# Experts' weights loaded 2 MB at a time, into a ring with two more 1 MB places

## The chip, the cores and the metric

The program runs on one core of a Trainium2 chip. The metric is the device time of one execution in microseconds, the median of several runs.

## The reference

Two transformer blocks follow each other on 256 tokens of 1024 features, in float32. The first has two layers of attention and MLP. The second mixes latent attention with a bidirectional mLSTM and ends in a layer of 16 experts, whose weights are the largest part of what is read:

```python
def ec_moe(x, w_router, w_e_gate, w_e_up, w_e_down):
    B, T, D = x.shape
    cap = CAP_FACTOR * T // N_EXPERTS
    aff = jax.nn.softmax((x @ w_router).astype(jnp.float32), axis=-1)
    g, idx = lax.top_k(aff.transpose(0, 2, 1), cap)
    xs = jax.vmap(lambda xb, ib: xb[ib])(x, idx)
    a = jnp.einsum('becd,edf->becf', xs, w_e_gate)
    u = jnp.einsum('becd,edf->becf', xs, w_e_up)
    y = jnp.einsum('becf,efd->becd', jax.nn.silu(a) * u, w_e_down) * g[..., None].astype(x.dtype)
    ...
```

Each of the 16 experts takes its 32 best tokens (cap = 32), and has three matrices of 1024 x 1024: 201 MB together, all of which is read once.

## The kernel before

**The parts.** The first block and the mixer of the second come first. Their weights arrive 1 MB at a time in the four buffers `wr` (`load_w`), ACT rounds them to a high part (`whi`), DVE or Pool takes the rest (`wlo`), and TensorE makes three products of each with the high and low parts of x. Then come the router and the experts.

**The experts.** They are worked in four groups of four (G4 = 0 to 3). Each group has 16 tiles of gate weights, 16 of up and 16 of down; a tile holds 128 rows and 512 columns of each of the four experts, 128 x 2048 floats or 1.049 MB. In all there are 192 tiles, numbered here 0 to 191 in the order in which they are used (`order_e`): 0 to 15 are the first group's gate, 16 to 31 its up, 32 to 47 its down, and so on. `product` makes four products of a tile, one per expert, with no rounding in between. TensorE's order is written by hand; the other engines' is set by a scheduler that keeps to the program's dependences.

**Between gate and up of the first group.** First only the rows of the first four experts are gathered (`xs0`), a feature tile ahead of each two gate tiles. After gate tile 15 the rows of the other twelve are gathered (`xsr`, eight feature tiles of 384 columns), then the slots' tokens are transposed (`ptr`) and their gates taken (`gsl`), and only then comes tile 16, the first of up.

**The ring of places.** `load_e` issues the loads of the tiles on SP's queue, in the order of use; each waits in that queue until the place that it goes to is free. `slots` names 23 places for the first 23 tiles, in the order in which they become free: the buffers of parts that are done. Some are whole (a row of a partition is 8 KB), some are put together of two halves of 4 KB rows (`("ew2.h0", "ew2.h4")`). From tile 23 on the places are used again in turn, `again`: all of them but the two that lie in `xsr` and the two named `once`, which other things need later. So 19 places go round, 14 whole and 5 halved:

```python
again = [s for s in slots if not any(p.startswith(("xsr", "once")) for p in s)]
...
s = slots[i] if i < len(slots) else again[(i - len(slots)) % len(again)]
```

**The end.** The last group's down tiles are laid out by columns, 128 at a time, so that little is left after the last load, which comes in four parts; then the last norm and four stores.

Of the kernel before, what the change touches and what calls it, by code (L numbers as in the profile page):

```python
# [16 lines left out]
PIECE = 512  # L17
# [25 lines left out]
LAST = (4, 2, 1, 1)  # L43
HP = 40
# [89 lines left out]
def lay_out(i):  # L134
# [10 lines left out]
    # the four rows of its block on each row  # L145
# [16 lines left out]
    # every q, then every k, then every v  # L162
# [27 lines left out]
    w = g["w_e_down_2"][0, 12:].reshape(4, 2, 4, 128, 8, 128).transpose(4, 1, 3, 2, 0, 5)  # L190
    o["w_e_down"][48:] = w.reshape(16, 128, 2048)
# [4 lines left out]
class Filler:  # L196
    """Matrix-product work that may run whenever the tensor engine would wait for another engine."""
# [42 lines left out]
def fused_kernel(ctx: ExitStack, tc: tile.TileContext, I, out):  # L240
# [26 lines left out]
    # brings the table of exp and tanh in while the first loads run  # L267
# [86 lines left out]
    def three(o, wh, wl, xh, xl, st, sp):  # L354
        mm(o, wh, xh, st, False)
        mm(o, wh, xl, False, False)
        mm(o, wl, xh, False, sp)

    def w_stationary(v, xs, o, small=0, ks=0, first=True, last=True):
        """o[:, m*256:(m+1)*256] (one bank) (+)= W[:, m-tile].T @ x over the contraction tiles of v"""  # L360
        xh, xl = xs
        K, n = v.shape[1], v.shape[2]
        for k0, k1, _, hv, lv in pieces(v, small):
            for k in range(k0, k1):
                for m in range(n // 128):
# [29 lines left out]
    def accumulate(w, dn, xh, xl, kx, first, last):  # L395
        """dn (8 output tiles in four banks) += W[two contraction tiles].T @ x[kx:kx+2]"""
        def one(k, m, hv, lv, m0, kk):
            ms = slice((m - m0) * 128, (m - m0 + 1) * 128)
            three(dn[m // 2][:, (m % 2) * 256:(m % 2) * 256 + 256], hv[:, kk, ms], lv[:, kk, ms], xh[:, kx + k],
                  xl[:, kx + k], first and k == 0 and m % 2 == 0, last and k == 1)  # L400

        if last:
            # finish one output tile after the other
# [20 lines left out]
    def heads_apart(u, d):  # L424
        """of two heads on 64 rows each: hi and lo above one another, hi where the head is"""
# [14 lines left out]
    def rstd_cols(ssum, n, nm, bank=None):  # L440
        """per token (partition) 1/sqrt(mean + eps), for the two token tiles"""
# [11 lines left out]
    def bcast_rows(col2, dst, bank=None):  # L453
        """dst[p, t*128 + s] = col2[s, t] on every partition"""
# [6 lines left out]
    def updated(dn):  # L461
        """x += dn, two tiles of features at a time"""
# [27 lines left out]
    with tc.tile_pool(name="memp", bufs=1) as mp:  # L490
# [15 lines left out]
        def mem_side(l, o, w):  # L506
            mh = mp.tile([128, 8, 256], FR, tag="mh", name="mh", bufs=2)
            ml = mp.tile([128, 8, 256], FR, tag="ml", name="ml", bufs=2)
            g = w_stationary(w, (mh, ml), o, 0 if l else 2)
# [4 lines left out]
            return mh, ml  # L514
# [36 lines left out]
    # ------------------------------------------------------------ first block  # L551
# [3 lines left out]
    def layer(l, lp, ap, start):  # L555
        hh, hl, ssum = start
        xs = (hh, hl)
        stat = {}

        # blocks of two heads, feature-major: the first kind's q, the second's, their k  # L560
# [4 lines left out]
        def tables():  # L565
            """the turns of q and k, with the norm's factor"""
# [10 lines left out]
        def turned(c, o):  # L577
            """rotates two blocks, each dimension with the one eight rows away"""
# [154 lines left out]
        def pv_dil():  # L733
# [3 lines left out]
            # the two heads in turn, each on its half of the columns of the array  # L737
# [86 lines left out]
        def project(mp_):  # L824
# [22 lines left out]
        for mp_ in range(4):  # L847
            project(mp_)
            if mp_:
                accumulate(load_w(I["w_out"][l, mp_ - 1]), dn, yh, yl, 2 * mp_ - 2, mp_ == 1, False)  # L850
        accumulate(load_w(I["w_out"][l, 3]), dn, yh, yl, 6, False, True)
        return dn

    def mlp(l, mp, side, dn):
        # what is used last lies where the last products' operands still are
        urs = [mp.tile([128, 2, 256], FT, name=f"ur{i}") for i in range(2)]
        uhs, uls = ([mp.tile([128, 2, 256], FR, name=f"u{n}{i}") for i in range(LAG + 1)] for n in "hl")
        hh, hl, ssum = split_and_sum(dn, ("g_mlp", l * 8), mp, () if l else HMQ)
# [4 lines left out]
        def up(c):  # L863
            o = acc_tile("up")
            return o, w_stationary(load_w(I["w_up"][l, c]), (hh, hl), o)

        def relu2(o):
            r = urs[nu[0] % 2]
            uh, ul = uhs[nu[0] % (LAG + 1)], uls[nu[0] % (LAG + 1)]
# [4 lines left out]
            return uh, ul  # L874
# [6 lines left out]
        for c in range(1, 16):  # L881
# [18 lines left out]
    def silu_row(v):  # L900
        """twice the silu"""
# [4 lines left out]
    def mod_rows(a, b, vs, mp):  # L906
        """columns of the modulation as sums along the rows of their weights"""
# [10 lines left out]
    def modulation(mp):  # L918
        """shift and scale of both sides"""
# [19 lines left out]
    # ------------------------------------------------------------ second block  # L939
# [14 lines left out]
    def modulated(src, rb, sc, sh, tp, emit, eng=None):  # L954
        """emit(k, t, shift column): h[k] = t + shift, t = src*rstd*scale"""
# [54 lines left out]
    def queries(xs, kpe, qn, qp, tp):  # L1010
# [4 lines left out]
        qh = tp.tile([128, 3, 256], FR, tag="qh", name="qh")  # L1015
        ql = tp.tile([128, 3, 256], FR, tag="ql", name="ql")
# [19 lines left out]
        for c in (2, 0, 1):  # L1036
# [24 lines left out]
    def gate_weights(wg, tp):  # L1061
        """the gates' weights for xc and xm themselves, through the blocks of q, k and v"""
# [15 lines left out]
        # q meets k through the product of their blocks  # L1078
# [13 lines left out]
    def diagonals(n, i):  # L1092
        """the 4x4 blocks of each tile of features on the diagonal of a square"""
# [78 lines left out]
    def log_gates(gt, gc, tp):  # L1172
        """gc: a, b, total, largest a"""
# [21 lines left out]
    def rows(gc, t):  # L1195
        """the rows a of a tile on every partition"""
# [783 lines left out]
```

## Time and profile before

| what | us |
|---|---|
| median of 3 runs | 1614.09 (1611.87 to 1615.5) |
| span of the profiled execution, first to last instruction | 1614.4 |
| TensorE busy (matrix products) | 1444.0 |
| DVE, ACT, Pool busy | 895.1, 674.2, 234.1 |

The page gives the profiled execution by its span; it has no other time of its own. A busy share is an average over parts with different limits, so the experts' part has to be read by itself: by the slices of the page, by windows and by timelines. In those the `gate`, `up` and `y` products read `ew`, the tile of weights; `ew` loads on SPq (SP's queue) are the experts' loads. A line L288 or L1660 is that of a helper, so groups are told apart by their tiles.

### The profile page before, as it was taken

How to read it: one execution, taken by the hardware profiler on the slowest of the kernel's cores; microseconds unless marked ns; L12 is line 12 of the kernel's file. 1: busy time of each engine (PE TensorE's matmuls, PEld its weight loads, DVE VectorE, ACT ScalarE, POOL GpSimd, SP SyncE). 2: the span in 40 equal slices, each digit the busy share in tenths (PEclk: the TensorE clock that was granted, in tenths of full speed). 3: DMA queues.
4: the chain of work that ended last, by engine and by line, in shares of the span. 5: the costliest groups of instructions: out<-in, count | busy, mean ns of one | idle time of the engine just before them, and what ended most of it. 6: DMA issues, size and time to landing. Idle time of an engine off the chain costs nothing.

```text
span 1614.4 us, 27279 instructions
## 1 busy us (share of the span) xinstructions
PE 1444.0 (89%) x10903; PEld 1153.8 (71%) x10903; DVE 895.1 (55%) x1609; ACT 674.2 (42%) x1339; POOL 234.1 (14%) x204
## 2 busy tenths in 40 slices
PE   8999999999999999999988999999798666766766
PEld 7999999999998998999987899878642100110114
DVE  7876688776886588897698875954410000000001
ACT  7555555555556556555565665544310000000001
POOL 3100022212210015322153101300100000000000
PEclk9999999999999999999999999999899788877787
DMA  8543446666443456767743322544889999999997
GB/s 310 186 142 131 158 170 254 243 227 217 183 157 115 160 196 229 273 253 273 274 162 111 132 79 98 196 183 156 339 345 416 419 419 418 418 417 417 419 418 320
DMA packets 67119, 404.89 MB, mean 251 GB/s; under 512 B 7344, under 2 KB 9264, under 8 KB 26544
## 3 DMA queue, kind: packets, MB, share of 16 engines
q1 hardware_dynamic: 66848, 403.04, 65.2%
q8 instruction: 85, 1.39, 0.3%
q14 instruction: 42, 0.34, 0.1%
q10 hardware_dynamic: 144, 0.11, 0.0%
HBM read 402.08 MB, written 1.05 MB: 250 GB/s over the span
## 4 chain that ended last, share of the span: by engine, by line
PE 61%; issue 29%; DVE 6%; ACT 2%; POOL 1%; DMA 0%; SPq 0%; POOLq 0%; ACTq 0%; DVEq 0%
PE dn L288 13%; PE up L288 10%; PE gate L288 9%; PE tanh L288 4%; PE z L288 4%; PE v L288 2%; PE prj L288 2%; DVE wlo L351 2%; PE scl L288 2%; PE wo L288 1%; PE sc L288 1%; DVE pre L1112 1%; PE xm L288 1%; PE S L288 1%; PE pvl L288 1%
## 5 line engine op out<-in xcount | busy, mean ns | idle before, releaser
L345 ACT CAST whi<-wr 128x512 fp32r<-128x512 f32 (+1 forms) x647 | 394.2, 616 | 366.7 <-PE up L288 81.1
L351 DVE TENSOR_TENSOR wlo<-wr,whi 128x512 fp32r<-128x512 f32 (+1 forms) x563 | 404.3, 728 | 158.5 <-ACT whi L345 156.3
L349 POOL TENSOR_TENSOR wlo<-wr,whi 128x512 fp32r<-128x512 f32 (+1 forms) x84 | 119.4, 1422 | 487.7 <-ACT whi L345 446.8
L288 PE MATMUL up<-hh,wlo 128*128 128x256 f32 x512 | 146.0, 285 | 6.0 <-DVE wlo L351 4.8
L288 PE MATMUL up<-hl,whi 128*128 128x256 f32 x512 | 145.6, 284 | 1.3 <-DVE hl L421 1.2
L1898 DVE TENSOR_TENSOR ehh<-up,ehh 128x512 f32<-128x512 f32 x8 | 5.5, 692 | 253.1 <-PE up L288 253.1
L288 PE MATMUL dn<-uh,wlo 128*128 128x256 f32 x512 | 145.3, 284 | 0.4 <-DVE wlo L351 0.4
L288 PE MATMUL up<-hh,whi 128*128 128x256 f32 x512 | 145.4, 284 | 0.2 <-ACT whi L345 0.2
L288 PE MATMUL dn<-uh,whi 128*128 128x256 f32 x512 | 145.0, 283 | 0.0
L288 PE MATMUL dn<-ul,whi 128*128 128x256 f32 x512 | 144.9, 283 | 0.0
L288 PE MATMUL y<-ew,ehl 128*32 128x128 f32 (+1 forms) x896 | 91.0, 512 | 39.5 <-DMA ew<-in_w_e_down_dram 38.6
L288 PE MATMUL up<-ew,xsr 128*32 128x512 f32 x384 | 82.1, 811 | 39.3 <-DMA ew<-in_w_e_up_dram 39.3
L288 PE MATMUL gate<-hh,whi 128*128 128x256 f32 x384 | 110.0, 286 | 0.0
L288 PE MATMUL gate<-hl,whi 128*128 128x256 f32 x384 | 108.6, 283 | 0.0
L288 PE MATMUL gate<-hh,wlo 128*128 128x256 f32 x384 | 108.6, 283 | 0.0
L288 PE MATMUL gate<-ew,xsr 128*32 128x512 f32 x384 | 71.0, 706 | 37.1 <-DMA ew<-in_w_e_gate_dram 36.7
L288 PEld LDWEIGHTS up<-hh,wlo 128*128 128x128 f32 x512 | 98.1, 192 | 8.1 <-DVE wlo L351 6.6
L288 PEld LDWEIGHTS up<-hl,whi 128*128 128x128 f32 x512 | 98.1, 192 | 2.4 <-DVE hl L421 2.1
L288 PEld LDWEIGHTS y<-ew,ehl 128*32 128x32 f32 x896 | 28.4, 128 | 99.0 <-DMA ew<-in_w_e_down_dram 77.4
L288 PEld LDWEIGHTS dn<-uh,wlo 128*128 128x128 f32 x512 | 98.3, 192 | 0.9 <-DVE wlo L351 0.8
L288 PEld LDWEIGHTS up<-hh,whi 128*128 128x128 f32 x512 | 98.1, 192 | 0.4 <-ACT whi L345 0.4
L288 PEld LDWEIGHTS dn<-uh,whi 128*128 128x128 f32 x512 | 98.3, 192 | 0.1
(531 smaller groups left out, 3477.9 us busy)
## 6 DMA issues: line engine op xcount, KB each, us to landing
ew<-in_w_e_down_dram SPq DMA_DIRECT2D x47, 1024.0 KB, 16.1
ew<-in_w_e_gate_dram SPq DMA_DIRECT2D x46, 1024.0 KB, 15.6
ew<-in_w_e_up_dram SPq DMA_DIRECT2D x46, 1024.0 KB, 15.7
wr<-in_w_up_dram SPq DMA_DIRECT2D x32, 1024.0 KB, 4.8
wr<-in_w_down_dram SPq DMA_DIRECT2D x32, 1024.0 KB, 5.9
wr<-in_w_gates_dram SPq DMA_DIRECT2D x24, 1024.0 KB, 4.8
wr<-in_w_modT_dram SPq DMA_DIRECT2D x24, 1024.0 KB, 4.9
wr<-in_w_in_dram SPq DMA_DIRECT2D x24, 1024.0 KB, 4.8
```

Source lines behind the costliest of these rows:

```text
L288: PE.matmul(o, l, r, start=st, stop=sp, skip_group_check=True)
L345: A.copy(hv, src)
L349: behind[1] = G.tensor_tensor(lv, src, hv.bitcast(FT), op=OP.subtract).ins
L351: behind[0] = V.tensor_tensor(lv, src, hv.bitcast(FT), op=OP.subtract).ins
L1112: V.scalar_tensor_tensor(pre, xm[:, k, w:w + 256], vc("cw", w * 8 + k), pre, op0=OP.mult, op1=OP.add)
L1898: V.tensor_tensor(h[:, c], up[j], h[:, c], op=OP.mult)
```

## The change

It does five things.

1. The program is built with `dynamic_dma_scratch_size=64`: the room that Pool's descriptors have in SBUF, which this kernel does not use, becomes free, 16 KB of each partition. A new pool `ew0` there holds two places of 1 MB, `("ew0.a/0",)` and `("ew0.a/1",)`, first in `slots`. `load_e(2)` fills them long before the other loads of experts, where the second block begins. So `slots` has 25 places.
2. Tiles of equal size that lay apart are made in pairs (`hi_lo`, `whl.w`, `x2p.xh`, `x2p.hx`, `yp.y`, `ew1.e`), so that two places of 1 MB lie side by side in each.
3. On the host, the experts' weights are laid out with two tiles side by side, 32 blocks of 128 x 4096, so that a partition's row of two tiles is 16 KB.
4. From tile 25 on only the five pairs of places in `again` are used, and two tiles are loaded by one transfer of 2 MB. Tile 25 itself, and the last four (`TAIL`), are loaded alone, the very last in four parts as before.
5. Comments and docstrings go. The helpers take the pair of hi and lo as one tile.

```diff
+TAIL = 4
...
     for n in ("gate", "up", "down"):
-        w = g["w_e_%s_2" % n][0].reshape(4, 4, 8, 128, 2, 512).transpose(0, 2, 4, 3, 1, 5)
-        o["w_e_" + n] = np.ascontiguousarray(w).reshape(64, 128, 2048)
+        w = g["w_e_%s_2" % n][0].reshape(4, 4, 8, 128, 2, 512).transpose(0, 2, 3, 4, 1, 5)
+        o["w_e_" + n] = np.ascontiguousarray(w).reshape(32, 128, 4096)
...
-    whi = whl.tile([128, WH * PIECE], FR, tag="whi", name="whi")
-    wlo = whl.tile([128, WH * PIECE], FR, tag="wlo", name="wlo")
+    whx = whl.tile([128, 2, WH * PIECE], FR, tag="w", name="wh")
+    whi, wlo = whx[:, 0], whx[:, 1]
...
+    def hi_lo(pl, K, tag, **kw):
+
+        t = pl.tile([128, 2, K, 256], FR, tag=tag, name=tag, **kw)
+        return t[:, 0], t[:, 1], t
...
-        load_e(2 + E1)
+        load_e(4 + E1)
...
+    slots = ([("ew0.a/0",), ("ew0.a/1",), ("yp.y/0",), ("yp.y/1",), ("ew1.e/0",), ("ew1.e/1",), ("ew1.f",)] +
+             [("ew2.h0", "ew2.h4"), ("ew2.h1", "ew2.h5"), ("ew2.h6",), ("ew2.h2", "ew2.h8"), ("cst.cbuf2", "ew2.h9"),
+              ("ew2.h3", "ew2.h10"), ("xsr.0",), ("ew2.h11", "xsr.1"), ("x2p.xh/0",), ("x2p.xh/1",)] +
+             [("wrp.wr",)] * WR + [("whl.w/0",), ("whl.w/1",), ("x2p.hx/1",), ("once.xT",)])
+
+    again = ["ew0.a", "yp.y", "ew1.e", "x2p.xh", "whl.w"]
...
+    def load_e(upto):
+        while len(ring) < min(upto, len(order_e)):
+            i = len(ring)
+            G4, n, q = order_e[i]
+            src = I["w_e_" + n][G4 * 8 + q // 2][:, q % 2 * 2048:q % 2 * 2048 + 2048]
+            if i < len(slots):
+                parts = slot_parts(i)
+                w = 2048 // len(parts)
+                for j, t in enumerate(parts):
+                    load_part(t, src[:, j * w:(j + 1) * w])
+                ring.append(parts)
+                continue
+            t = halves(again[(i - len(slots) + 1) // 2 % len(again)])
+            if q % 2 == 0 and i < len(order_e) - TAIL:
+                load_part(t.rearrange("p a n -> p (a n)"), I["w_e_" + n][G4 * 8 + q // 2])
+                ring.extend([[t[:, 0]], [t[:, 1]]])
+            else:
+                parts = [t[:, q % 2]]
...
+    pools["ew0"] = pool(yst, "ew0", "right")
+    yp = pools["yp"] = pool(yst, "yp", "right")
+    load_e(2)
...
-    nc = _bacc.Bacc("TRN2", target_bir_lowering=False, num_devices=1)
+    nc = _bacc.Bacc("TRN2", target_bir_lowering=False, num_devices=1, dynamic_dma_scratch_size=64)
```

**Where the loads stand: the first places used again.** SP's queue, before, from the last tile of the first filling (`xT`, tile 22) on. A number behind `ew` is the place's; `128x1024` is a half.

```order
L1660 DMA xT_84<-in_w_e_up_dram 128x2048 [waits DMAHW5_49,DVE_49,PE_49]
L1660 DMA ew_12892<-in_w_e_up_dram 128x2048 [waits DMAHW6_49,PE_49]
L1660 DMA ew_12898<-in_w_e_up_dram 128x2048 [waits DMAHW7_49,PE_49]
L1660 DMA ew_12904<-in_w_e_up_dram 128x2048 [waits DMAHW0_49,PE_49]
L1660 DMA ew_12910<-in_w_e_up_dram 128x2048 [waits DMAHW1_49,PE_49]
L1660 DMA ew_12940<-in_w_e_up_dram 128x2048 [waits DMAHW2_49,PE_49]
L1660 DMA ew_12946<-in_w_e_up_dram 128x1024 [waits DMAHW3_49,PE_49]
```

The same place of SP's queue now, from the last tile of the first filling (`xT`, tile 24) on. ew_9091 is `ew0.a`, ew_11737 `yp.y`, ew_11740 `ew1.e`, ew_12414 `x2p.xh`, ew_12624 `whl.w`.

```order
L1492 DMA xT_84<-in_w_e_up_dram 128x2048 [waits DMAHW7_49,DVE_49,PE_49]
L1492 DMA ew_9091<-in_w_e_up_dram 128x2048 [waits DMAHW0_49,PE_49]
L1492 DMA ew_11737<-in_w_e_up_dram 128x4096 [waits DMAHW1_49,PE_49]
L1492 DMA ew_11740<-in_w_e_up_dram 128x4096 [waits DMAHW2_49,PE_49]
L1492 DMA ew_12414<-in_w_e_up_dram 128x4096 [waits DMAHW3_49,PE_49]
L1492 DMA ew_12624<-in_w_e_down_dram 128x4096 [waits DMAHW5_49,DMAHW4_49,PE_49]
L1492 DMA ew_9091<-in_w_e_down_dram 128x4096 [waits DMAHW0_49,PE_49]
```

Before, a new place per tile, each that of the next tile used. Now tile 25 goes alone, tiles 26 and 27 to `yp.y`, 28 and 29 to `ew1.e`, 30 and 31 to `x2p.xh`, 32 and 33 to `whl.w`, 34 and 35 to `ew0.a` again.

**Who reads those places.** TensorE, now, from the last gate tile (15) to the second up tile (17).

```order
L289 MATMUL gate1_12678<-ew_12414,xs0_12676 32x512 x4
L289 MATMUL xs_12776<-P_12671,ew_12627 128x384 x2
...
L289 MATMUL xs_12804<-P_12671,ew_12627 128x384 x2
L1870 MATMUL ptr_12809<-cbuf_81,P_12671 128x128 x4
L1870 MATMUL ptr_12815<-cbuf_81,P_12671 128x128 x4
L289 MATMUL gsl_12821<-aff_12641,P_12671 128x4 x8
L289 MATMUL up0_12833<-ew_12414,xs0_12676 32x512 x4
L289 MATMUL up1_12834<-ew_12616,xs0_12676 32x512 x4
```

And before, at the same point.

```order
L288 MATMUL gate1_12703<-ew_12639,xs0_12701 32x512 x4
L288 MATMUL xs_12801<-P_12696,ht_12671 128x384 x2
...
L288 MATMUL gsl_12848<-aff_12665,P_12696 128x4 x8
L288 MATMUL up0_12860<-ew_12641,xs0_12701 32x512 x4
L288 MATMUL up1_12861<-ew_12643,xs0_12701 32x512 x4
```

TensorE's order is the same. The two halves of `x2p.xh` (ew_12414) now hold tile 15 and tile 16, on either side of the gathers; before, tile 15 lay in a buffer of `wr` of its own.

**The two early loads.** SP's queue now, where the second block begins; before, the same rows stand there without the two of `ew_9091`.

```order
L316 DMA wr_9193<-in_w_in2_dram 128x2048 [waits DMAHW2_49,DVE_49,Pool_49]
L316 DMA wr_9280<-in_w_in2_dram 128x2048 [waits DMAHW3_49,DVE_49]
L316 DMA wr_9355<-in_w_in2_dram 128x8x128 [waits DMAHW4_49,DVE_49]
L1492 DMA ew_9091<-in_w_e_gate_dram 128x2048 [waits DVE_49]
L1492 DMA ew_9091<-in_w_e_gate_dram 128x2048
L316 DMA wr_9401<-in_w_ukv_dram 128x2048 [waits DMAHW5_49,DVE_49,Pool_49]
```

On ACT two activations of silu (L1892 before, on `gate`) now stand among the eight copies of the gathers into `xsr`, instead of behind them.

## Rows read from the trace of the kernel before

**Rows 1.** The page's 40 slices of 40.4 us: DMA busy tenths, GB/s.
```profile
DMA  8543446666443456767743322544889999999997
GB/s 310 186 142 131 158 170 254 243 227 217 183 157 115 160 196 229 273 253 273 274 162 111 132 79 98 196 183 156 339 345 416 419 419 418 418 417 417 419 418 320
```

**Rows 2.** Waits of TensorE from 1000 us: us in total, times, longest.
```profile
PE up L288 <- DMA ew<-in_w_e_up_dram: 39.3, 53, 2.4
PE y L288 <- DMA ew<-in_w_e_down_dram: 38.6, 42, 1.9
PE gate L288 <- DMA ew<-in_w_e_gate_dram: 36.7, 48, 1.6
```

**Rows 3.** Windows: rows of 8 KB alone, of 4 KB alone, the whole stream.
```profile
core 0: us, PE busy (x) PEld busy (x) DVE busy (x) ACT busy (x) POOL busy (x), PEclk, DMA share, GB/s
...
1255.00:1282.00 27.00, 17.43 (x94) 2.62 (x92) 0.00 (x0) 0.53 (x1) 0.00 (x0) 0.81 1.01 421
...
1389.00:1395.00 6.00, 4.10 (x20) 0.59 (x20) 0.00 (x0) 0.00 (x0) 0.00 (x0) 1.00 1.02 408
1176.40:1604.30 427.90, 309.91 (x2034) 79.65 (x2033) 20.90 (x34) 17.80 (x34) 0.00 (x0) 0.84 1.01 415
```

**Rows 4.** Timeline of SP's queue: start, us, what; the last first filling, the first reuse.
```profile
1159.12 0.33 SPq L1660 DMA_DIRECT2D xT<-in_w_e_up_dram  x1
1175.36 14.14 SPq L1660 DMA_DIRECT2D ew<-in_w_e_up_dram  x12
```

**Rows 5.** Windows of 5 us around the start of the stream.
```profile
1165.00:1170.00 5.00, 0.00 (x0) 0.00 (x0) 4.72 (x12) 0.00 (x0) 1.01 (x1) 0.50 0.39 165
1170.00:1175.00 5.00, 4.16 (x18) 2.53 (x22) 2.05 (x6) 0.46 (x1) 0.00 (x0) 0.50 0.00 0
1175.00:1180.00 5.00, 5.00 (x44) 1.87 (x40) 0.41 (x1) 0.46 (x1) 0.00 (x0) 0.99 0.74 254
1185.00:1190.00 5.00, 5.00 (x44) 1.88 (x40) 0.41 (x1) 0.46 (x1) 0.00 (x0) 1.00 1.00 407
1190.00:1195.00 5.00, 5.00 (x35) 2.09 (x28) 0.63 (x1) 0.00 (x0) 0.00 (x0) 1.00 1.00 366
```

**Rows 6.** Timeline of the end: the last product of experts, the stores.
```profile
1604.62 1.08 PE L288 MATMUL y<-ew,ehl 128*32 128x128 f32 x32
...
1609.18 1.81 SPq L1957 DMA_DIRECT2D out_dram<-yo  x4
```

**Rows 7.** Timeline of TensorE, first group: start, us; a tile is 8 records.
```profile
1173.45 2.70 PE L288 MATMUL gate<-ew,xs 128*32 128x512 f32 x16
...
1176.72 1.92 PE L288 MATMUL gate<-ew,xs 128*32 128x512 f32 x16
...
1179.22 1.92 PE L288 MATMUL gate<-ew,xs 128*32 128x512 f32 x16
...
1192.77 10.59 PE L288 MATMUL xs<-P,ht 128*128 128x384 f32 x32
...
1204.61 1.93 PE L288 MATMUL gsl<-aff,P 128*128 128x4 f32 x16
1206.81 5.36 PE L288 MATMUL up<-ew,xs 128*32 128x512 f32 x48 [0.27 <-DVE gs L1852]
...
1224.84 11.37 PE L288 MATMUL y<-ew,ehl 128*32 128x512 f32 x104
1237.22 1.06 PE L288 MATMUL y<-ew,ehl 128*32 128x512 f32 x8 [1.01 <-DMA ew<-in_w_e_down_dram]
```

**Rows 8.** SP's queue and a window where the second block begins.
```profile
798.46 11.45 SPq L315 DMA_DIRECT2D wr<-in_w_in_dram  x4
813.21 0.34 SPq L315 DMA_DIRECT2D wr<-in_w_ukv_dram  x1
...
800.00:820.00 20.00, 19.39 (x162) 19.19 (x161) 16.50 (x27) 11.21 (x24) 9.21 (x9) 1.00 0.66 233
```

**Rows 9.** Groups of ACT by line and form, 1290 to 1615 us: count, busy, mean ns.
```profile
L1892 ACT ACTIVATE ehh<-gate 128x512 f32<-128x512 f32 x4 | 2.4, 597 | 158.2 <-PE gate L288 158.2
```

More of the change, by code (lines that the diff above doesn't have):

```diff
@@ L366, in w_stationary @@
                     ms = slice(m * 128, (m + 1) * 128)
-                    three(o[:, m * 256:(m + 1) * 256], hv[:, k - k0, ms], lv[:, k - k0, ms], xh[:, ks + k],
-                          xl[:, ks + k], first and k == 0 and m == 0, last and k == K - 1)
+                    three(o[:, m * 256:(m + 1) * 256], hv[:, k - k0, ms], lv[:, k - k0, ms], x2[:, :, ks + k],
+                          first and k == 0 and m == 0, last and k == K - 1)
                 yield 0.33 * (n // 128)
     def x_stationary(v, xs, os_, ks=None, first=True, last=True):
-        xh, xl = xs
+        xh, xl = xs[:2]
         K, n = v.shape[1], v.shape[2]
@@ L393, in out_banks, with accumulate @@
         return [dw[j // 2][:, (j % 2) * 512:(j % 2) * 512 + 512] for j in range(4)]
-    def accumulate(w, dn, xh, xl, kx, first, last):
+    def accumulate(w, dn, x2, kx, first, last):
         def one(k, m, hv, lv, m0, kk):
             ms = slice((m - m0) * 128, (m - m0 + 1) * 128)
-            three(dn[m // 2][:, (m % 2) * 256:(m % 2) * 256 + 256], hv[:, kk, ms], lv[:, kk, ms], xh[:, kx + k],
-                  xl[:, kx + k], first and k == 0 and m % 2 == 0, last and k == 1)
+            three(dn[m // 2][:, (m % 2) * 256:(m % 2) * 256 + 256], hv[:, kk, ms], lv[:, kk, ms], x2[:, :, kx + k],
+                  first and k == 0 and m % 2 == 0, last and k == 1)
         if last:
@@ L856, in mlp @@
         urs = [mp.tile([128, 2, 256], FT, name=f"ur{i}") for i in range(2)]
-        uhs, uls = ([mp.tile([128, 2, 256], FR, name=f"u{n}{i}") for i in range(LAG + 1)] for n in "hl")
-        hh, hl, ssum = split_and_sum(dn, ("g_mlp", l * 8), mp, () if l else HMQ)
+        us = [hi_lo(mp, 2, f"ux{i}") for i in range(LAG + 1)]
+        xs, ssum = split_and_sum(dn, ("g_mlp", l * 8), mp, () if l else HMQ)
         rb = mp.tile([128, 256], FT, name="rb")
@@ L873, in relu2 @@
             split_x(r, uh, ul)
-            return uh, ul
+            return ux
         o, g = up(0)
@@ new lines, in fused_kernel, with halves, slot_parts @@
+    again = ["ew0.a", "yp.y", "ew1.e", "x2p.xh", "whl.w"]
+    held = {}
+    last_load = []
+    two = {}
+    def halves(n):
+        if n not in two:
+            p, tag = n.split(".")
+            two[n] = pools[p].tile([128, 2, 2048], FT, tag=tag, name="ew")
+        return two[n]
+    def slot_parts(i):
+        s = slots[i]
+        parts = []
+        for n in s:
+            p, tag = n.split(".")
+            if n in held:
+                t = held.pop(n)
+            elif n == "xsr.0":
+                held["xsr.1"] = rt.tile([128, 3072], FT, tag="xsr", name="ew")
+                t, held["xsr.1"] = held["xsr.1"][:, :2048], held["xsr.1"][:, 2048:]
+            elif n == "once.xT":
+                t = xT.rearrange("p k n -> p (k n)")
+            elif "/" in n:
+                t = halves(n[:-2])[:, int(n[-1])]
+            else:
+                t = pools[p].tile([128, 2048 // len(s)], FT, tag=tag, name="ew")
+            parts.append(t)
+        return parts
@@ new lines, in load_part @@
+    def load_part(dst, src):
+        with tc.issue_after(last_load[0].ins) if last_load else ExitStack():
+            last_load[:] = [nc.sync.dma_start(out=dst, in_=src)]
+    def load_e(upto):
[14 more added lines that the diff above has]
+                ring.extend([[t[:, 0]], [t[:, 1]]])
+            else:
+                parts = [t[:, q % 2]]
+                if i == len(order_e) - 1:
+                    parts = [parts[0][:, a:a + 512] for a in range(0, 2048, 512)]
+                w = 2048 // len(parts)
+                for j, p in enumerate(parts):
+                    load_part(p, src[:, j * w:(j + 1) * w])
+                ring.append(parts)
@@ L1571, in fused_kernel @@
             G.tensor_tensor(xT[:, k], xT[:, k], rb1, op=OP.mult)
-    xc = x2p.tile([128, 8, 256], FT, tag="xc", name="xc")
-    hm = x2p.tile([128, 2, 1024], FT, tag="hm", name="hm")
-    tzg = [yp.tile([128, 8, 256], FT, tag=n, name="t" + n) for n in ("yh", "yl")]
+    xh_ = x2p.tile([128, 2, 2048], FT, tag="xh", name="xh")
+    xc = xh_[:, 0].rearrange("p (k n) -> p k n", k=8)
+    hm = xh_[:, 1].rearrange("p (t n) -> p t n", t=2)
+    tz_ = yp.tile([128, 2, 8, 256], FT, tag="y", name="tzg")
+    tzg = [tz_[:, i] for i in range(2)]
     with ExitStack() as es:
@@ L1619, in fused_kernel @@
         F.need(g2)
[L1621 to L1661 removed]
     pools["ew1"] = pool(ctx, "ew1", "right")
[L1664 removed]
+    tga = xc
     with ExitStack() as es:
[L1666 removed]
+        ys = hi_lo(x2p, 8, "hx")
         m = mla(xs, qn, qp, hm, tga, ys, pool(es, "b2l"))
@@ L1747, in fused_kernel @@
     V.tensor_tensor(aff, aff, den[:, :, None].to_broadcast([128, 2, 16]), op=OP.mult)
-    ht = x2p.tile([128, 2, 1024], FT, tag="hh", name="ht")
+    ht = halves("x2p.hx")[:, 0].rearrange("p (t n) -> p t n", t=2)
     with tc.issue_after(ex.ins):
@@ L1829, in fused_kernel @@
         scaled(d, o, xsr[:, d])
-    eb = [x2p.tile([128, 2, 1024], FT, tag=n, name="e" + n) for n in ("hh", "hl")]
+    eb = [halves("x2p.hx")[:, i].rearrange("p (t n) -> p t n", t=2) for i in range(2)]
     h, PT, ye = eb[0][:, 0], eb[0][:, 1], eb[1][:, 0]
```

117 lines of the change are left out of this document (35 added, 82 removed).

## Prediction

> **What bounds the kernel now.** I read the 40 slices of the page first [rows 1]. Up to slice 30 the rate changes from slice to slice; from slice 31 (1211 us) on the load stream runs at 416 to 419 GB/s, but for the last slice. This is the experts' part: 192 tiles of weights of 1.049 MB (201 MB), each used once. The waits of TensorE say the same [rows 2]: 39.3 + 38.6 + 36.7 = 114.6 us go to weights that have not landed. So the end is set by the load stream: when it starts for good, how fast it runs, whether it is ever empty. TensorE is not the limit: 310 us busy in the 428 us of the stream [rows 3].
>
> The stream has two parts. 23 tiles are loaded ahead, into 23 places, while earlier work runs; the last goes out at 1159.1 us, and then SP stands still until 1175.4, when the product of tile 0 gives back the first place [rows 4]. In between the DMA engines are empty [rows 5]: nothing from about 1167 to 1176.3 us (a busy share of 0.74 in the slice to 1180). From 1176.3 until the last product, at 1604.6 [rows 6], the other 169 tiles run: 428.3 us, **2.534 us a tile**. Behind it lie 9.8 us of finish to the end of the span, 1614.4, which the change leaves as they are. The span of this execution stands 0.3 us above the median of the runs, 1614.09.
>
> **What a row costs.** A place in one piece takes rows of 8 KB, one in two halves rows of 4 KB. The windows that hold only one kind run at 421 and 408 GB/s [rows 3], so 2.490 and 2.570 us a tile: halving the number of rows saved 0.08 us. In the steady cycle of 19 places 14 are whole and 5 halved: 2.511 us, or 424.4 us for 169 tiles. The stream took 3.9 us more: about 0.8 in the dips to 407 and 366 GB/s at 1185 to 1195 [rows 5], the rest (3.1) landing and the slowest engine at the end.
>
> **The change part by part.**
>
> *Two more places.* The first filling holds 25 tiles instead of 23; the two new places are filled long before. 167 tiles remain: -2 x 2.534 = **-5.1 us**.
>
> *Rows of 16 KB.* No row of this trace has such a load in this queue. If a row has a fixed cost, the next halving saves half of the last one: 0.04, so 2.450 us a tile. Bounds: 2.490 (nothing more is saved) and 2.410 (the same 0.08 again); worse than 2.490 has no neighbour, since longer rows were faster here. I take 2.450, the middle, by the fixed cost. The last four tiles keep 8 KB rows. Against 2.511: 163 x 0.061 + 4 x 0.021 = **-10.0 us**, bounds -3.5 and -16.5.
>
> The Trainium skill (DMA: Bandwidth & Descriptors, Where 436 GB/s comes from) puts the ceiling of the ports at 435 GB/s, which is 2.41 us a tile. By that rate instead of mine the time would be 163 x 0.04 = 6.5 us less; no row here comes above 421 over a long window.
>
> *Where the 2 MB loads may go.* Here the change gives something back. Before, 19 of the 23 places are used again, in the order in which their tiles are used. Now only five places of 2 MB are, ten tiles; the others are filled once. The SP order shows it: tile 25 goes to the second half of the first place (ew_9091), tiles 26 to 29 to ew_11737 and ew_11740, tiles 30 and 31 to ew_12414. The last of these held tiles 15 and 16, and the PE order shows that between the products of these two stand all the gathers of the other experts' rows. The times [rows 7]: tiles 0 and 1 are done at 1176.15 (1173.45 + 2.70), 2 and 3 at 1178.6, 4 and 5 at 1181.1, about 1.25 us a tile; tile 16 only after the gathers (10.6 us from 1192.8) and the slots' gates (from 1204.6): the row from 1206.81 is six tiles in 5.36 us, so tile 16 is done at 1207.7. Before, the places of tiles 0 to 10 and 13 to 15, 14 tiles or 35 us of loads, came back ahead of that, and the stream never emptied. After, the places of tiles 1 to 5 do: five tiles.
>
> So the stream now goes: from issue to busy engines 0.9 us (1175.4 to 1176.3), so tile 25 starts at 1176.15 + 0.9 = 1177.1, **+0.8** against 1176.3; five tiles, 2.49 + 4 x 2.45 = 12.3 us, end at 1189.4; the next starts at 1207.7 + 0.9 = 1208.6. **+19.2 us** of empty engines. Tiles 32 and 33 need tiles 21 and 22 used (1213.0, +0.9 = 1213.9) while tiles 30 and 31 end at 1213.5: **+0.4**. After that the places come back ahead: tiles 36 and 37 land near 1228.6, where TensorE, at 0.9 us a tile from 1224.84, has just used tile 35; from then on every 2 MB that is used frees a place while four more, 19.6 us of loads, are in the queue, and the two products take 1.8 us at the full clock and about twice that at half (the mean granted clock of the stream is 0.84 [rows 3]). The dips of 0.8 us lay in the stretch that is now empty: **-0.8**.
>
> *The two early loads.* They stand in SP's queue behind four loads of the second block's weights and ahead of w_ukv, and wait for DVE's sum of the modulation, which follows the last modT tile that the load before them waits for. The fourth of those loads goes out by 809.9 us, the next at 813.2, and the engines are 0.66 busy [rows 8]. w_ukv lands up to 2 x 2.49 = 5.0 us later; with four places for these weights it is asked for ahead of use, so I take nothing, bounds 0 and +5.0.
>
> *Silu moved on ACT.* Two activations of 0.6 us [rows 9] now stand among the copies of the gathers, on which tile 16 waits. TensorE fills one bank while the other is emptied, 1.3 us a gather; I take 0, bounds 0 and +1.2.
>
> *hi and lo in one tile, fewer issues.* The engines' instructions are the same one for one, apart from names; nothing. Fewer issues on SP gain nothing: it waits for places.
>
> **Sum:** -5.1 - 10.0 + 0.8 + 19.2 + 0.4 - 0.8 = +4.5 us on 1614.4, so 1618.9; **1619 us**. The change saves 15 us and pays 19 for them.
>
> **The rivals.**
>
> *No empty stretch* (faster). If the places came back in time, or the part from 1176 to 1208 were covered by something I read wrongly, the sum without 19.2 and 0.4 and with the dips back is -14.3: 1600 us. For it: the engines were kept busy there before. Against: the SP order names the place, the PE order the product. Chance 0.12.
>
> *Rows of 16 KB at 2.410* (no change). The empty stretch stays, the rows save 16.5: 1612.4 us, inside 0.2%. For it: the step from 4 to 8 KB was 0.08. Against: a fixed cost per row halves. Chance 0.22. (The ceiling of the Trainium skill's page, above, lies at this rate.)
>
> *Rows of 16 KB save nothing beyond 8 KB* (slower still). 1625.4 us. For it: 421 GB/s may already be what the memory gives. Chance 0.15.
>
> *The early loads hold back w_ukv.* 1624 us, if TensorE then waits for these weights near 820 us; in that part it waits rather for DVE. Chance 0.05.
>
> *The two places are not gained* (the change does not do what it says). The first filling in the SP order has 25 tiles, so this is all but excluded: 0.01, at 1624.
>
> **How the numbers follow.** The likeliest case, +4.5, has 0.45; its own range, with ACT's bound and the rates between, is 1616 to 1622, a quarter of it inside 0.2%. 0.2% (3.2 us) is about what a measurement of this kernel tells from no change; the three runs of before lie 3.6 us apart. Slower: 0.34 + 0.15 + 0.06 = 0.55. Same: 0.11 + 0.18 of the second rival = 0.29. Faster: 0.12 + 0.04 = 0.16. The range takes in the second and third rival with their edges, 1607 to 1628, and leaves out the first.
>
> **What would show it.** After: a stretch of some 19 us with 0 GB/s between about 1190 and 1208 us, and SP waiting that long for TensorE's product of an up tile; TensorE waiting for weights from about 1228 instead of 1237 us; from 1214 on a stream of about 428 GB/s in windows of 25 us (421: third rival, 435: second), never empty; the early loads landing near 820 us with the same waits of TensorE there. If the stretch is not empty, the step on the places is wrong; if it is and the time still falls, the rate is.

## The result: slower, by a little more than forecast

| kernel | median, us | against before |
|---|---|---|
| before, on the same chip | 1614.80 (1611.87 to 1617.04, 4 runs) | |
| changed | 1623.93 (1622.8 to 1625.66, 4 runs) | 1.0055, 95% [1.004, 1.007] |
| changed, a second time on another chip | 1623.35 (before there 1617.23) | 1.0040, [1.0026, 1.0054] |

The forecast was 1619, slower, by a sum of +4.5 us. By the medians it is +9.1 us on the first chip (by the interval 6.5 to 11.3, so the 4.5 lies below it) and +6.1 on the second (4.2 to 8.7). In the profiled executions the span went from 1614.4 to 1621.8 us, +7.4. A time and a span are not the same number: where an execution has both, the time is 1.8 us the longer (1623.6 for 1621.8). By that, the execution of before that was profiled lay about 1.4 us above its median, which is why the spans differ by less than the medians.

The 40 slices of the changed kernel, of 40.5 us each:

```profile
DMA  8533447665543456777753323544749999999997
GB/s 309 186 139 130 158 169 259 233 237 209 182 156 128 152 195 224 283 259 280 266 203 120 108 80 110 208 156 178 315 193 425 428 427 428 428 428 428 427 428 315
```

Against [rows 1] two things differ in the experts' part: the slice from 1176 to 1216 us (thirtieth number) fell from 345 to 193 GB/s, and behind it the stream runs at 425 to 428 GB/s, not 416 to 419. The change gives and takes where the prediction put it. Windows of 5 us through the thirtieth slice and a little beyond, as in [rows 5], with the GB/s last:

```profile
1175.00:1180.00 5.00, 5.00 (x40) 1.77 (x36) 0.41 (x1) 0.32 (x1) 0.00 (x0) 0.95 0.48 144
1180.00:1185.00 5.00, 5.00 (x44) 1.88 (x40) 0.41 (x1) 0.47 (x2) 0.00 (x0) 1.00 1.02 419
1185.00:1190.00 5.00, 5.00 (x44) 1.88 (x40) 0.41 (x1) 0.47 (x2) 0.00 (x0) 1.00 1.03 436
1190.00:1195.00 5.00, 5.00 (x38) 1.99 (x31) 0.27 (x1) 0.12 (x1) 0.00 (x0) 1.00 0.13 54
1195.00:1200.00 5.00, 5.00 (x17) 2.89 (x16) 1.19 (x3) 3.22 (x4) 0.00 (x0) 1.00 0.00 0
1200.00:1205.00 5.00, 4.67 (x21) 2.87 (x19) 1.24 (x2) 2.41 (x4) 0.00 (x0) 1.00 0.00 0
1205.00:1210.00 5.00, 4.73 (x46) 2.75 (x48) 0.34 (x2) 0.58 (x1) 0.00 (x0) 1.00 0.22 43
1210.00:1215.00 5.00, 5.00 (x52) 1.51 (x48) 0.00 (x0) 0.00 (x0) 0.00 (x0) 1.00 0.96 383
1215.00:1220.00 5.00, 4.76 (x44) 2.26 (x40) 0.00 (x0) 2.15 (x4) 0.00 (x0) 1.00 0.95 380
1220.00:1225.00 5.00, 4.65 (x44) 1.74 (x36) 1.38 (x2) 0.58 (x1) 0.00 (x0) 1.00 1.00 418
```

The first four windows hold 5 x (144 + 419 + 436 + 54) = 5.27 MB, which is five tiles (5.24 MB). Windows of 2 us show both edges of what follows:

```profile
1190.00:1192.00 2.00, 2.00 (x24) 0.65 (x20) 0.00 (x0) 0.12 (x1) 0.00 (x0) 1.00 0.32 135
...
1208.00:1210.00 2.00, 2.00 (x24) 0.65 (x20) 0.00 (x0) 0.00 (x0) 0.00 (x0) 1.00 0.55 106
1210.00:1212.00 2.00, 2.00 (x24) 0.60 (x20) 0.00 (x0) 0.00 (x0) 0.00 (x0) 1.00 0.82 311
```

Between them nothing moves. In windows of half a us the last weights come by 1191.0 and the next from 1209.0, so the engines are empty for 18 us, while TensorE is 4.7 to 5.0 us busy in each 5. That is the empty stretch. The queue's own timeline shows where it stood; the first two rows are the early loads:

```profile
810.72 1.01 SPq L1492 DMA_DIRECT2D ew<-in_w_e_gate_dram  x2
813.05 0.33 SPq L316 DMA_DIRECT2D wr<-in_w_ukv_dram  x1
...
1159.40 0.33 SPq L1492 DMA_DIRECT2D xT<-in_w_e_up_dram  x1
1176.58 32.04 SPq L1492 DMA_DIRECT2D ew<-in_w_e_up_dram  x4
1213.45 21.55 SPq L1492 DMA_DIRECT2D ew<-in_w_e_down_dram  x8
```

Four loads (tile 25, then three pairs) take from 1176.58 to 1208.62 us to go out, the fourth from 1208.30 on, and the longest wait of the queue is 26.3 us for an up product:

```profile
SPq L1492 <- PE up L289: 107.6, 30, 26.3
SPq L1492 <- PE gate L289: 91.4, 27, 16.8
```

TensorE's timeline, as in [rows 7]:

```profile
1173.74 2.77 PE L289 MATMUL gate<-ew,xs 128*32 128x512 f32 x16
...
1193.13 10.59 PE L289 MATMUL xs<-P,ew 128*128 128x384 f32 x32
...
1204.48 0.66 PE L1870 MATMUL ptr<-cbuf,P 128*128 128x128 f32 x4 [0.33 <-ACT xsr L1840]
1204.98 1.93 PE L289 MATMUL gsl<-aff,P 128*128 128x4 f32 x16
1207.17 7.07 PE L289 MATMUL up<-ew,xs 128*32 128x512 f32 x64 [0.27 <-DVE gs L1880]
...
1227.32 1.93 PE L289 MATMUL y<-ew 128*32 128x512 f32 x16 [0.22 <-DMA ew<-in_w_e_down_dram]
1232.22 2.41 PE L289 MATMUL y<-ew 128*32 128x512 f32 x16 [2.98 <-DMA ew<-in_w_e_down_dram]
```

Eight tiles in the row of 7.07 us: tile 16 is done at 1207.17 + 0.88 = 1208.05, and 0.25 us later the queue moves on, at 1208.30. The first wait for weights comes at 1227.3, not 1237.2. The steady stream, to be held against [rows 3]:

```profile
1255.00:1282.00 27.00, 18.95 (x92) 4.42 (x96) 1.50 (x2) 0.00 (x0) 0.00 (x0) 0.73 1.01 428
...
1215.00:1600.00 385.00, 231.77 (x1573) 58.57 (x1566) 13.55 (x19) 8.07 (x14) 0.00 (x0) 0.79 1.01 427
```

TensorE's waits for weights, as in [rows 2]:

```profile
PE y L289 <- DMA ew<-in_w_e_down_dram: 59.0, 28, 4.6
PE up L289 <- DMA ew<-in_w_e_up_dram: 50.8, 24, 3.1
PE gate L289 <- DMA ew<-in_w_e_gate_dram: 43.2, 21, 4.5
```

They are 153.0 us, 38 more than before, while the end came 7 us later. Tiles now land in twos, so there are half as many waits and each is longer. Of an engine that is not the limit, such a sum does not say what is lost.

### The profile page after: what moved, and what is told of

Read it like the earlier page. It is cut to its first block, busy times and chain, and to the rows that moved or that the text cites. A ratio compares the mean times of both kernels' runs of the same rounds, so it can differ in the third digit from the quotient of the medians.

```text
span 1621.8 us, 27014 instructions
## 1 busy us (share of the span) xinstructions
PE 1411.9 (87%) x10903; PEld 1154.3 (71%) x10903; DVE 895.3 (55%) x1609; ACT 674.3 (42%) x1339; POOL 234.2 (14%) x204
## 4 chain that ended last, share of the span: by engine, by line
PE 61%; issue 29%; DVE 6%; ACT 1%; POOL 1%; DMA 0%; SPq 0%; POOLq 0%; ACTq 0%; DVEq 0%
PE dn L289 13%; PE up L289 10%; PE gate L289 9%; PE tanh L289 4%; PE z L289 4%; PE v L289 2%; PE prj L289 2%; DVE wh L352 2%; PE scl L289 2%; PE wo L289 1%; DVE pre L1111 1%; PE sc L289 1%; PE xm L289 1%; PE S L289 1%; PE pvl L289 1%
## 5 line engine op out<-in xcount | busy, mean ns | idle before, releaser
L346 ACT CAST wh<-wr 128x512 fp32r<-128x512 f32 (+1 forms) x647 | 393.9, 616 | 366.8 <-PE up L289 81.7
L352 DVE TENSOR_TENSOR wh<-wr,wh 128x512 fp32r<-128x512 f32 (+1 forms) x563 | 404.7, 729 | 159.0 <-ACT wh L346 157.0
L289 PE MATMUL up<-hx,wh 128*128 128x256 f32 x1536 | 194.2, 284 | 7.8 <-DVE wh L352 5.1
L289 PEld LDWEIGHTS up<-hx,wh 128*128 128x128 f32 x1536 | 187.6, 192 | 11.0 <-DVE wh L352 6.8
L289 PE MATMUL dn<-ux,wh 128*128 128x256 f32 x1536 | 189.7, 283 | 0.4 <-DVE wh L352 0.4
L350 POOL TENSOR_TENSOR wh<-wr,wh 128x512 fp32r<-128x512 f32 (+1 forms) x84 | 118.7, 1413 | 488.6 <-ACT wh L346 453.5
L289 PEld LDWEIGHTS dn<-ux,wh 128*128 128x128 f32 x1536 | 186.6, 192 | 1.0 <-DVE wh L352 0.8
L289 PE MATMUL gate<-hx,wh 128*128 128x256 f32 x1152 | 142.0, 284 | 0.0
L289 PEld LDWEIGHTS gate<-hx,wh 128*128 128x128 f32 x1152 | 139.1, 192 | 1.9 <-issue 1.4
L289 PE MATMUL y<-ew 128*32 128x128 f32 (+1 forms) x896 | 83.5, 519 | 59.7 <-DMA ew<-in_w_e_down_dram 59.0
```

What stands on the lines that cost most here:

```text
L289: PE.matmul(o, l, r, start=st, stop=sp, skip_group_check=True)
L346: A.copy(hv, src)
L350: behind[1] = G.tensor_tensor(lv, src, hv.bitcast(FT), op=OP.subtract).ins
L352: behind[0] = V.tensor_tensor(lv, src, hv.bitcast(FT), op=OP.subtract).ins
```

## Experiments

Theory A was the prediction's: the empty stretch takes what places and rows give. Its rival B: the loss lies in the 2 MB loads or in a ring of only ten tiles later on. Each chip has its own runs of before: 1616.18 us for the first four kernels, 1617.23 for the next four, 1615.01 for the last two.

**Four and eight tiles bridged.** Beside the ten places that still go round, fifteen stand unused after their first tile. The edit loads some tiles into places that are already free, the first half of `ew0.a` and some of these fifteen (here eight tiles; the other kernel has the first four):

```diff
+    BRIDGE = [('ew0.a/0',), ('ew1.f',), ('ew2.h0', 'ew2.h4'), ('ew2.h1', 'ew2.h5'), ('ew2.h6',), ('ew2.h2', 'ew2.h8'), ('cst.cbuf2', 'ew2.h9'), ('ew2.h3', 'ew2.h10')]
...
+            if 30 <= i < 30 + len(BRIDGE):
+                parts = place(BRIDGE[i - 30])
+                w = 2048 // len(parts)
+                for j, t in enumerate(parts):
+                    load_part(t, src[:, j * w:(j + 1) * w])
+                ring.append(parts)
+                continue
-            t = halves(again[(i - len(slots) + 1) // 2 % len(again)])
+            t = halves(again[(i - (len(BRIDGE) if i >= 30 else 0) - len(slots) + 1) // 2 % len(again)])
```

Expected of eight:

> The changed kernel, but tiles 30 to 37 are loaded 1 MB each into eight places that are already given back (those of tiles 0 and 6 to 12); the pairs go on from tile 38. All else of the change stays: 25 places at first, 16 KB rows from tile 38 on. Theory A (the empty stretch of 17 us between 1192 and 1209 us is what the change loses): the stretch goes, every later load comes about 17 us earlier: about 1607 us, 17 less than the changed kernel and 8 less than the kernel before; TensorE's waits for weights grow by about as much as the end does not fall. Theory B (the stretch is harmless, the loss lies in 2 MB transfers or in a ring of only ten tiles later on): no change to speak of, 1621 to 1627 us, and the stream has new gaps after 1230 us.

Measured: 1607.96 us, 0.9950 [0.9938, 0.9963], 8.2 under before, as A said. B falls: the same 2 MB loads and the same ten places go on behind. One part of A's expectation did not come: TensorE's waits for weights did not grow but fell, to 140.1 us.

Expected of four:

> As the kernel with eight such tiles, but with four only (30 to 33). Theory A: four tiles of 2.5 us fill 10 of the 17 us: the engines stand empty for about 7 us, the end comes at about 1614 us, half way between the changed kernel and the one with eight. Theory B: 1621 to 1627 us, as for eight.

Measured: 1616.25 us, 1.0002 [0.9992, 1.0013], no different from before; A had it 0.8 us under (1614, where before was 1614.8). The windows with four tiles show why it is not better:

```profile
1195.00:1200.00 5.00, 5.00 (x17) 3.00 (x16) 1.24 (x2) 2.51 (x4) 0.00 (x0) 1.00 0.72 288
1200.00:1205.00 5.00, 4.41 (x33) 3.36 (x35) 1.02 (x3) 2.33 (x4) 0.00 (x0) 1.00 0.00 0
1205.00:1210.00 5.00, 5.00 (x52) 1.50 (x48) 0.00 (x0) 0.00 (x0) 0.00 (x0) 1.00 0.67 213
...
1215.00:1220.00 5.00, 4.76 (x44) 2.06 (x46) 0.00 (x0) 2.15 (x4) 0.00 (x0) 1.00 0.62 249
1220.00:1225.00 5.00, 4.65 (x44) 1.71 (x40) 2.08 (x3) 0.59 (x1) 0.00 (x0) 1.00 0.74 249
```

The first three lose 5 x (3 - (288 + 213) / 427) = 9.1 us, about as expected with a restart, but a second hole of 2 x 5 x (1 - 249/427) = 4.2 us has come, since a later pair now goes to `ew0.a`, whose first half tile 30 has filled again, and tile 30 is used near the end of the up products, some 14 us after tile 16. With eight tiles the same hole has 3.4 us:

```profile
1195.00:1200.00 5.00, 5.00 (x17) 2.90 (x16) 1.35 (x2) 3.22 (x4) 0.00 (x0) 1.00 1.01 410
1220.00:1225.00 5.00, 4.88 (x44) 1.46 (x36) 1.25 (x2) 0.50 (x2) 0.00 (x0) 1.00 0.62 203
1225.00:1230.00 5.00, 4.77 (x45) 1.75 (x48) 0.82 (x2) 0.59 (x1) 0.00 (x0) 1.00 0.86 360
```

**Twelve tiles bridged.** Four more, tiles 40 to 43, go to the buffers of `wr`:

```diff
-('ew2.h3', 'ew2.h10')]
+('ew2.h3', 'ew2.h10'), ('wrp.wr',), ('wrp.wr',), ('wrp.wr',), ('wrp.wr',)]
...
-            if 30 <= i < 30 + len(BRIDGE):
-                parts = place(BRIDGE[i - 30])
+            k = i - 30 if i < 38 else i - 32
+            if 30 <= i < 38 or 40 <= i < 44:
+                parts = place(BRIDGE[k])
...
-            t = halves(again[(i - (len(BRIDGE) if i >= 30 else 0) - len(slots) + 1) // 2 % len(again)])
+            t = halves(again[(i - (0 if i < 30 else 8 if i < 40 else 12) - len(slots) + 1) // 2 % len(again)])
```

> The kernel with eight tiles in free places still has a hole of 3.4 us in the stream at 1220 to 1228 us (203 and 360 GB/s in two 5 us windows), since tiles 42 and 43 go to a place whose tile 30 is only used at 1222 us. Here four more tiles, 40 to 43, go 1 MB each to the four buffers of wr, free with tiles 17 to 20, so that tile 44 waits for tile 22 and tile 46 for tile 30. Theory A (each us in which the engines stand empty costs one at the end): the hole goes, 3.4 less than the kernel with eight, so 11.6 us less than the kernel before: about 1604.6 us where before is at 1616.2. Rival: the hole is covered by something later, and the time stays 8.2 us below the kernel before, at 1608.

Measured: 1603.83 us, 0.9917 [0.9905, 0.993], and on a third chip 0.9926 [0.9911, 0.9941]: 13.4 and 11.4 us under before, where A had 11.6 and its rival 8.2, which both intervals exclude. No hole is left:

```profile
1205.00:1210.00 5.00, 4.73 (x46) 2.25 (x48) 0.34 (x2) 0.12 (x1) 0.00 (x0) 1.00 1.03 414
1220.00:1225.00 5.00, 4.65 (x42) 1.65 (x37) 1.74 (x3) 0.59 (x1) 0.00 (x0) 1.00 1.01 418
1225.00:1230.00 5.00, 5.00 (x52) 1.56 (x48) 0.34 (x1) 0.00 (x0) 0.00 (x0) 1.00 1.03 439
1255.00:1282.00 27.00, 15.75 (x96) 2.88 (x92) 0.00 (x0) 1.19 (x2) 0.00 (x0) 0.73 1.01 427
```

It is the version that beats both: 13.4 us under before, and 19.5 under the changed kernel on the same chip.

**The two places alone.** The 23 old places and the two of `ew0` hold the first 25 tiles, and 21 of them go round, one tile at a time:

```diff
+    singles = [s for s in slots if not any(p.startswith(("xsr", "once", "x2p.hx")) or p == "ew2.h11" for p in s)]
...
-            t = halves(again[(i - len(slots) + 1) // 2 % len(again)])
...
+            parts = place(singles[(i - len(slots)) % len(singles)])
```

> The two more places alone: 25 places at first, and then 21 of them go round in turn, 1 MB a load with rows of 8 or 4 KB, as the kernel before does with 19. Theory P (two tiles fewer remain for the stream): 2 x 2.534 = 5.1 us less than before, 1609.7 us; no empty stretch at 1192 us. Rival Q (the stream starts later by as much, or the early loads cost it elsewhere): 1614.8 us, as before.

Measured: 1610.94 us, 0.9968 [0.9956, 0.998], 5.2 less. P holds, and since the early loads, the moved silu and the pairs of tiles are all in this kernel, none of them costs more than these runs could tell (2 us, half the interval).

**The empty stretch put in.** To the last kernel one line is added, so that the seventh load of the ring goes to the place of tile 16:

```diff
+    singles.insert(6, singles.pop(singles.index(("x2p.xh/1",))))
```

> The two places alone (1 MB loads, all places in turn), with one thing changed: the seventh load of the ring, tile 31, goes to the place of tile 16 in place of that of tile 6, and the order is otherwise as it was. So the empty stretch is put in, without 2 MB loads and without a ring of ten tiles. Theory A: six tiles end at about 1192 us, the next starts at 1208.6: about 16.5 us empty, and 16.5 us more at the end: 1627 us, 11.3 more than the kernel before, where the two places alone are 5.2 below it. Theory B (the loss in the changed kernel belongs to 2 MB loads or to the short ring): at most a few us more than the two places alone, 1611 to 1615 us.

Measured: 1627.58 us, 1.0070 [1.0057, 1.0083], 10.4 over before. Against the two places alone that is 1.0070 / 0.9968 = 1.0102, 16.5 us (by the two intervals, 3 either way). A says 16.5; that the two agree to a tenth is chance, with 3 us either way. B, at most a few us, falls. The stretch, with single tiles and a ring of 21:

```profile
1190.00:1195.00 5.00, 5.00 (x23) 2.77 (x15) 1.12 (x2) 1.72 (x2) 0.00 (x0) 1.00 0.01 5
1195.00:1200.00 5.00, 5.00 (x17) 3.01 (x16) 1.19 (x3) 2.17 (x4) 0.00 (x0) 1.00 0.00 0
1200.00:1205.00 5.00, 4.41 (x36) 3.28 (x38) 0.74 (x3) 2.33 (x4) 0.00 (x0) 1.00 0.00 0
1205.00:1210.00 5.00, 5.00 (x52) 1.44 (x45) 0.00 (x0) 0.00 (x0) 0.00 (x0) 1.00 0.72 239
```

Taken out with one kernel and put in with another, it has its price both times.

**The length of a row.** The same 2 MB loads, but the tiles lie one by one on the host:

```diff
+def apart(w):
+    return np.ascontiguousarray(w.reshape(32, 128, 2, 2048).transpose(0, 2, 1, 3)).reshape(64, 128, 2048)
...
-            src = I["w_e_" + n][G4 * 8 + q // 2][:, q % 2 * 2048:q % 2 * 2048 + 2048]
+            src = I["w_e_" + n][G4 * 16 + q]
...
-                load_part(t.rearrange("p a n -> p (a n)"), I["w_e_" + n][G4 * 8 + q // 2])
+                load_part(t, I["w_e_" + n][G4 * 16 + q:G4 * 16 + q + 2].rearrange("a p n -> p a n"))
```

> The changed kernel with the tiles laid out on the host as before it, one by one: each 2 MB transfer takes two rows of 8 KB per partition in place of one of 16 KB; same transfers, same places, same waits. Theory R (the length of a row sets the rate): 421 GB/s in the stream from 1215 to 1600 us in place of 427, 162 tiles x 0.04 us = 6.5 us more, about 1630 us. Rival S (the size of a transfer or the small number of them sets it): 427 GB/s and 1624 us, as the changed kernel.

Measured: 1627.94 us, 1.0075 [1.006, 1.009]: by the ratios only 3 us over the changed kernel, which had run on another chip. So both were run side by side:

> The changed kernel itself, beside the others on one chip: 9 us above the kernel before, 1625 us where that is at 1616. It serves as the mark for the next one.

> The changed kernel with 8 KB rows again, now beside the changed kernel on one chip. In the first look its stream ran at 421 GB/s, but its median stood only 2.7 us over where the changed kernel would be by its ratio from another chip, and the first place came back 1.5 us earlier in the profiled execution. Theory R: 162 tiles x 0.04 = 6.5 us over the changed kernel, less about 1 that the start of the stream gives back with shorter rows: 5 to 6.5 us. Rival: 2.7 us or less, so part of the rate is paid back somewhere after the stream.

Measured: 1623.35 (6.1 over before, not 9) and 1627.22, so 3.9 us for the shorter rows. That lies between the two guesses, and with 3 us either way by the two intervals it does not tell them apart. The rate is plain; 8 KB rows, then 16 KB rows, in the side-by-side runs:

```profile
1255.00:1282.00 27.00, 17.18 (x96) 4.25 (x100) 1.50 (x2) 0.00 (x0) 0.00 (x0) 0.87 1.01 421
```

```profile
1255.00:1282.00 27.00, 17.07 (x92) 4.28 (x96) 1.50 (x2) 0.00 (x0) 0.00 (x0) 0.85 1.01 428
```

421 GB/s is what 1 MB loads with such rows had before [rows 3]. Rival S, the size of the transfer, is out. A table of the Trainium skill (DMA: Bandwidth & Descriptors, Measured), for loads that GpSimd issues, has 341 GB/s for 1 MB and 425 for 16 MB. In this queue, with loads behind each other, doubling the load at equal rows changes nothing (421 GB/s for 1 MB and for 2 MB).

Of 6.5 us the profiled executions show 4.7 from the first load of the ring to the last product (1176.24 to 1611.65 against 1175.45 to 1615.57). One piece of the rest is the end: with 16 KB rows the 12 us ahead of the last product move 0.4 to 0.5 MB less, about a us. In the changed kernel:

```profile
1599.94:1604.94 5.00, 5.00 (x96) 3.13 (x98) 1.38 (x2) 1.38 (x4) 0.00 (x0) 0.78 1.00 410
1604.94:1609.94 5.00, 3.53 (x84) 2.41 (x72) 1.69 (x4) 0.95 (x4) 0.00 (x0) 1.00 0.83 324
1609.94:1611.94 2.00, 1.65 (x36) 1.36 (x36) 0.00 (x0) 0.11 (x1) 0.00 (x0) 1.00 0.17 64
```

**The end of the stream.** Is that due to the long rows shortly before the end? In the kernel with twelve bridged tiles, `TAIL` was set to 12:

```diff
-TAIL = 4
+TAIL = 12
```

> The kernel with twelve tiles in free places, but the last twelve tiles are loaded 1 MB at a time with 8 KB rows, not only the last four. In the 12 us that end with the last product, the kernel before moved 4.18 MB (421, 353 and 155 GB/s over 5, 5 and 2 us), the two with 8 KB rows 4.18 and 4.21 MB, those with 16 KB rows 3.69 to 3.80 MB. Theory T (2 MB loads with 16 KB rows shortly before the end make the stream run out unevenly, worth 0.9 us): these 12 us move 4.1 to 4.2 MB again; the time falls by 0.9 - 8 x 0.04 = 0.6 us, less than the runs can tell. Rival (the rate near the end has nothing to do with the rows of the last few loads): 3.7 to 3.8 MB as without the edit.

> The same kernel with twelve tiles in free places and four single loads at the end, as the mark beside the one with twelve: 13 us below the kernel before, and 3.7 to 3.8 MB in the last 12 us by either theory.

Measured: 1603.41 us, 0.9927 [0.9913, 0.9941], and 1603.60 us, 0.9926. The 12 us moved 4.17 MB with twelve single loads, and 4.16 with four. So the mark was not where the expectation had it, and Theory T's premise fell. The 3.69 MB in it came from windows placed 1.5 us too late; in the right place the earlier run of that kernel has 4.30. The times, 0.2 us apart, say nothing either way. Over all the kernels here:

| last 12 us, MB | kernels |
|---|---|
| 3.71 to 3.80 | changed (two runs); the stretch put in |
| 4.01, 4.04 | four, eight bridged |
| 4.16 to 4.32 | before; 8 KB rows (two runs); two places alone; twelve bridged (two runs); twelve single loads at the end |

The stretch put in has 8 and 4 KB rows and yet stands in the first line. What sets this us at the end stays open.

## Why the prediction was right, and where it was short

- **Two more places, -5.1 us.** 5.2 measured. Right.
- **Rows of 16 KB, 2.450 us a tile.** 427 to 428 GB/s are 2.456 to 2.450 us. The rate is right, and the second and third rival fall with it, 2.410 and 2.490. What it is worth at the end is less sure: of the 6.5 us between rows of 8 and 16 KB the kernels side by side showed 3.9, by 3 either way. The 163 tiles were 162, since tile 25 is loaded alone too; that is 0.04 us. The ceiling of the ports in the Trainium skill (DMA: Bandwidth & Descriptors, Where 436 GB/s comes from), 435 GB/s, was reached in no long window (windows of 5 us have up to 439).
- **The empty stretch, +19.2.** Place, cause and price right: putting such a stretch in cost 16.5 us, by 3 either way, where A said 16.5. In the changed kernel it was 18 us: the five tiles ahead of it took until 1191.0 rather than 1189.4, which changes nothing, since the restart is set by tile 16 and not by them, and the engines started at 1209.0 for 1208.6. Taking it out was worth 1 - 0.9917 / 1.0040 = 1.2%, 19.8 us, again by 3 either way. The sum has 19.2 + 0.4 for it, less 0.9 for the bridged tiles' shorter rows (seven of 8 KB, five of 4 KB), which is 18.7. The first rival, no empty stretch, said -14.3; the kernel made for it has -13.4 and, on another chip, -11.4.
- **The restart: +0.4 in all for the wait for tiles 21 and 22.** Too small: this is the step that fell short. I had the engines at their full rate from 1208.6 on but for 0.4 us. Up to 1225 they moved 5 x (43 + 383 + 380 + 418) = 6.12 MB, where 16.4 us at 428 are 7.02: 2.1 us lost. Of these, 0.35 is tile 16 being used later (1208.05 for 1207.7), with the early part of TensorE 0.3 us later in this execution. About 1.1 is the slow start: the windows of 2 us from 1208 have 106 and 311 GB/s, 0.83 MB, which at 428 take 1.95 us, so the full rate counts from 1210.05 and not from 1208.05 + 0.9 = 1208.95. I had read the 0.9 us off the busy share of the engines, 0.74 in the first 5 us of the stream before [rows 5], but the same row has 254 GB/s, which at 421 is 3.0 us of work and not 3.7: the engines were busy there but not yet at their rate. The start before had lost 0.7 us in this way, which my sum kept unseen in its rest of 3.1. The last 0.65 us is what the 0.4 stood for: the queue sent one load at 1208.30 and the next only at 1213.45. That this wait is the cause of the lower rate behind it was not tried.
- **The dips, -0.8.** The row of 366 GB/s at 1190 to 1195 [rows 5] is gone, as put in.
- **Nothing more at the end.** The last product came 7.3 us later (1604.62 [rows 6] to 1611.94), not 4.5. Of the missing 2.8, the restart has 1.0: the 2.1 less the 0.4 put in and less the 0.7 that the start before had lost. The last 12 us have 0.9: 3.80 MB for the 4.18 of before (421, 353 and 155 GB/s), by 0.42 MB a us; the end was put in as unchanged. The stream between 1225 and 1599.94 has 0.6: 160.22 MB, which is 427.3 GB/s and not 428. These are single executions; the medians' +9.1 and +6.1 cannot be split so finely.
- **The span read as a time.** I put the profiled execution of before 0.3 us above the median. That set a span against times; by the 1.8 us between the two it was about 1.4 above.
- **Early loads, silu, names: 0.** Right: w_ukv goes out at 813.05 for 813.21 [rows 8], TensorE's waits from 795 to 850 us are the same in both traces, from the first gather of `xsr` to tile 16 it takes 14.0 us in both (1193.13 to 1207.17, 1192.77 to 1206.81 [rows 7]), and the kernel with the places alone has the whole 5.2.

## What to carry to other kernels

When places are joined into bigger ones, write down for each the product that frees it and the time of that product: a queue in order stands at the first place that comes free late, and here places that came free over 15 us earlier (before 1193 us, against 1208) lay unused. Here a load stream that was the limit paid for each us in which it was empty (16.5 us for a stretch of about 16), and a little more for the restart. The gain of longer rows can be had without that loss, by sending a few loads to the old places until the joined ones come free.

## What was not expected of the hardware

The rate of this queue of loads went by the length of a row: 408 and 421 GB/s for 4 and 8 KB [rows 3] and 428 for 16 KB, the second doubling saving half of what the first did. At 8 KB it made no difference whether a load had 1 MB or 2 MB; the rows of 4 KB came in loads of 0.5 MB only, so there the two were not told apart. After an empty stretch the engines were busy well before they were at their rate: the first two windows of 2 us had 106 and 311 GB/s, at busy shares of 0.55 and 0.82. The last 12 us of the stream carry between 3.7 and 4.3 MB from kernel to kernel, a difference of 1.4 us for which no cause was found.
